# Output projection with odd-k weight buffers, early gate rows, samples' decays taken later; new beginning; operands at other SBUF addresses

## The chip, the cores and the metric

One Trainium2 chip, one of its cores. The metric is the device time of one launch in microseconds; the kernel before was run three times, and its time is the median of them.

## What is computed

One layer of a hybrid decoder, on 1024 prompt tokens and 8 samples of 8 tokens (T = 1088 columns in all), width D = 1024, everything in float32. Cut to what matters:

```python
mod = silu(c) @ w_ada + b_ada                     # (9, 6 * 1024): 1 prompt row, 8 sample rows
sh1, sc1, g1, sh2, sc2, g2 = split(mod, 6)
h = rms_norm(x, norm_mix_pre) * (1 + sc1) + sh1
proj = h @ w_in                                   # 6688 columns: z, x/B/C, dt, q, k, v, gate, beta, alpha
y = gated_rms_norm(ssd(causal_conv(x/B/C), dt))   # Mamba-2, 16 heads of 64, chunked scan
o = gated_rms_norm(delta_net(causal_conv(q, k, v), beta, alpha))   # 8 heads of 128
m = concat(y, o) @ w_out                          # 2048 x 1024
x = x + g1 * rms_norm(m, norm_mix_post)
h = rms_norm(x, norm_ffn_pre) * (1 + sc2) + sh2
f = (silu(h @ w_gate) * (h @ w_up)) @ w_down      # DFF = 2816
x = x + g2 * rms_norm(f, norm_ffn_post)
```

The samples start from given states and convolution halos; the prompt starts from zero. The new states are outputs too.

## The kernel before

**Precision.** Every large product is three matmuls: both operands are split into a rounded high part and a low rest (`hh`/`hl` or `sh`/`sl` for activations, `wh`/`wl` for weights), and high x high, low x high and high x low are summed in PSUM. `load_half` (L167 to L173) loads a 128x512 piece of weights `wr` on SP's DMA queue; `split_half` (L161 to L166) makes `wh` by a cast on ACT (L164) and `wl` by a subtraction on DVE (L165). Pool `wp` has four buffers of each.

**Stages.** (1) Start: the adaLN blocks 0, 2, 1, 3 of 512 columns (`ada_block`, L268), norm of the nine token tiles (`norm_x`), transposing and modulating into the hidden columns `hh`, `hl` in three groups TH of 384, 384 and 320 columns (`hidden`, L353; its transposes are L320), and the first two tiles of the input projection, K and Q, beside it (`first_half`, L401, matmuls L408 to L410; for the other groups L189 to L191). (2) The GDN stage to about 750 us, (3) the SSD stage to about 998 us: the input projection runs tile by tile (`gemm`, L185), with recurrences beside it. (4) w_out, 998 to 1268 us: `gemm_rows` (L1325) goes over three groups of three token tiles; for each k (8 to 15, then 0 to 7) it takes a piece of the mixed rows (`mixed_piece`, `mx`), splits it into `sh`, `sl`, loads two halves of w_out and issues 18 matmuls (L1335, L1337, L1338). (5) FFN-up, 1270 to 1720 us, in a Strassen-like scheme of seven block products (L1815 to L1817, 272 columns each; the blocks are allocated in `blocks`, L1580). (6) w_down, 1720 us to the end.

**Order of the work.** Side work is written as Python generators (`spawn`) that go on by a step at each `tick()`; `wait(n)` lets n ticks pass. A tick comes after some matmuls of the running tile, so `wait` sets behind how many matmuls something is issued. PE's order is the order in which the program text issues (a manual schedule on PE alone). The order on ACT, DVE, POOL and SP's queue is decided by a scheduler when the program is built, with `tc.high_priority` as a hint; each engine then executes its list in order.

**Side work the change touches.** `params`, `halos` (the convolution halos of the samples, L366; five loads through one buffer `vT`, transposed at L373), `rates` (decay rates; its first product is L522), `ada_rest` (L635): the other eight adaLN blocks during the GDN stage, whose sums go to DRAM (`pdr`). `rows_late` (L1274) reads `pdr` back in w_out and makes the gate rows `gaindr` (L1301) and the FFN's `modT` (L1313) from it. `decays(j)` (L1033) loads and exponentiates the decays `L` of SSD head pair j; `ssd_pair(j)` (L1052) calls it for j + 1 before its own `xd`, `xe` (L1073, L1074; matmul L1091). `gdn_samples` (L1409) does the eight delta-net heads of the samples beside w_out, after `rows_late` (`beside`). It begins with

```python
sp.dma_start(out=d0, in_=accr[16:24, NP:T].partition_broadcast(NS))
dve.tensor_tensor(out=d0, in0=d0, in1=acs[0:NS, NC, 16:24]...)      # L1423
dve.tensor_scalar(out=d0, in0=d0, scalar1=0.0, ...)                 # L1425
act.activation(out=d0, in_=d0, func=AF.Exp)                         # L1426
yield from wait(3)
```

where `d0` is `s_d` in the profile, and then for each head h loads the state S0 (`s_S`), builds the operand `kb`, issues the products `pk` (L1512) and `pw` (L1520), scales S0 by eight end decays on POOL (L1527), and issues the product `po` (L1530).

Of the kernel before, what the change touches and what calls it, by code (L numbers as in the profile page):

```python
# [16 lines left out]
P = 128  # L17
D = 1024
# [25 lines left out]
def hybrid_step(ctx: ExitStack, tc: tile.TileContext, x_p, x_s, c_p, c_s, st_ssd, st_ssdc, st_gdn, st_gdnc,  # L44
# [30 lines left out]
    pdr = tc.dram_tile([P, 4 * D], F32, name="pdr")  # L75
# [3 lines left out]

    ident = const.tile([P, P], F32, name="ident")  # L80
# [24 lines left out]
    sels = const.tile([P, 4, 9], F32, name="sels")  # L105
    for i in range(4):
        dve.tensor_tensor(out=sels[:, i, :], in0=fold[:, 0:9], in1=ident[:, 9 + i:10 + i].to_broadcast([P, 9]),
                          op=ALU.add)
# [59 lines left out]
    def load_half(src, low=dve):  # L168
# [4 lines left out]
        return split_half(wr, low)  # L173
# [82 lines left out]
    for i in range(3):  # L256
        load_x(i, act)
# [40 lines left out]

    def params():
        act.dma_start(out=r1[0:8, :], in_=n_mix_pre[0].rearrange("(r c) -> r c", c=P))  # L300
        act.dma_start(out=r1[8:16, :], in_=n_ffn_pre[0].rearrange("(r c) -> r c", c=P))
        act.dma_start(out=r1[16:24, :], in_=ssd_nw[0].rearrange("(r c) -> r c", c=P))
        act.dma_start(out=r1[24:25, :], in_=gdn_nw)
        act.dma_start(out=r1[25:37, :], in_=ssd_cb[0].rearrange("(r c) -> r c", c=P))
        act.dma_start(out=r1[37:85, :], in_=ssd_cw[0].rearrange("j (r c) -> (j r) c", c=P))
        act.dma_start(out=r2, in_=gdn_cw[0].rearrange("j (r c) -> (j r) c", c=P))
        yield from wait(3)
# [4 lines left out]
        dve.tensor_copy(prm2T, ps[:, 128:224])  # L312

# [39 lines left out]
    def hidden(g, step, ks=range(KD)):  # L353
        c0, n = TH[g]
        for k in ks:
            ps = turned(g, k)
            modulated(ps, k, c0, n, hh[k][:, c0:c0 + n], hl[k][:, c0:c0 + n], init,
                      pool if k % 2 else dve)
            if k % step == step - 1:
                yield  # L360
        if KD - 1 in ks:
            hid_box[g] = clock[0]


    def halos():
        for src, a, n in ((st_ssdc[0], 0, 8), (st_ssdc[0], 8, 4), (st_gdnc[0], 0, 8), (st_gdnc[0], 8, 8),  # L366
                          (st_gdnc[0], 16, 8)):
            st = gk.tile([P, NP], F32, name="vT", bufs=1)[0:24, 0:n * P]
            act.dma_start(out=st, in_=src[:, :, a * P:(a + n) * P].rearrange("b t c -> (b t) c"))
# [8 lines left out]

    def hidden_rest():
        for i in range(3, NT):  # L380
            norm_x(i)
        yield from wait(5)
        yield from hidden(1, 3)
        yield from hidden(2, 3)
# [1529 lines left out]
```

## Time and profile before

| | us |
|---|---|
| runs | 2026.26, 2027.66, 2016.43; median 2026.26 |
| the profiled execution | 2017.53 |
| its span | 2015.8 |
| PE busy | 1951.3 (97%) |
| VectorE (DVE) busy | 1356.6 (67%) |
| ScalarE (ACT) busy | 1014.1 (50%) |
| GpSimd (POOL) busy | 138.7 (7%) |
| mean granted TensorE clock | 0.99 of full |

The span is the stretch from the first to the last instruction; the execution's own time has 1.7 us more around it. PE is TensorE's matmuls, PEld its weight loads, SPq the queue on which the Sync engine issues DMAs. A line number is that of the kernel before; a matmul row reads `out<-stationary or moving operands`, and in brackets stands how long the engine was idle before an instruction and what released it.

### The profile page before, as it was taken

Reading aid. Unit: us, or ns where it says so; the run is one execution under the profiler, and the core shown is the slowest. Engines: PE = TensorE matmul, PEld = TensorE weight load, DVE = VectorE, ACT = ScalarE, POOL = GpSimd, SP = SyncE. Lnnn points to the kernel's source line nnn. Section 1 sums busy time; section 2 is a strip of 40 time slices with the busy share of each in tenths; the row PEclk is TensorE's granted clock in tenths of the full one; section 3 lists DMA queues with packets and bytes.
Section 4 is the critical chain, followed back from the end, with each engine's and each line's share of the span. In section 5 each row is a group of like instructions: output and inputs, shape, how many; then the busy total and the mean of one; then the engine's idle time right before and its main releaser. Section 6 shows DMA issues by size and latency. Waiting matters only on the chain.

```text
span 2015.8 us, 35469 instructions
## 1 busy us (share of the span) xinstructions
PE 1951.3 (97%) x13211; PEld 1752.5 (87%) x13211; DVE 1356.6 (67%) x2949; ACT 1014.1 (50%) x2515; POOL 138.7 (7%) x188
## 2 busy tenths in 40 slices
PE   6999999999999999999989999999999999999998
PEld 4888999999999998998857677899999999988886
DVE  4768677877887656867648777885555556645465
ACT  3555445555555447767424556753333334444454
POOL 2110000000000001010002210100000000000000
PEclk8999999999999999999989999999999999999999
DMA  9133223333221237545376866422222223633131
GB/s 315 40 92 92 84 92 98 108 95 99 84 58 55 69 92 201 159 121 155 113 218 193 253 203 194 140 75 81 73 78 81 75 82 124 225 125 113 46 100 50
DMA packets 224764, 239.49 MB, mean 119 GB/s; under 512 B 19128, under 2 KB 177387, under 8 KB 224461
## 3 DMA queue, kind: packets, MB, share of 16 engines
q1 hardware_dynamic: 218203, 231.88, 37.2%
q10 hardware_dynamic: 6386, 5.33, 0.8%
q8 instruction: 104, 1.70, 0.4%
q14 instruction: 71, 0.58, 0.1%
HBM read 190.93 MB, written 46.25 MB: 118 GB/s over the span
## 4 chain that ended last, share of the span: by engine, by line
PE 79%; DVE 9%; DMA 6%; ACT 3%; issue 2%; POOL 0%; SPq 0%; DVEq 0%; POOLq 0%; ACTq 0%
PE ps L189 8%; PE ps L190 8%; PE ps L191 8%; PE ps L1815 7%; PE ps L1817 7%; PE ps L1816 7%; PE ps L1335 7%; PE ps L1338 6%; PE ps L1337 6%; PE ps L671 2%; PE ps L725 1%; DMA L<-accr 1%; DVE tm L827 1%; DVE rr L829 1%; DMA mx<-mixdr 1%
## 5 line engine op out<-in xcount | busy, mean ns | idle before, releaser
L189 PE MATMUL ps<-hh,wh 128*128 128x384 f32 (+1 forms) x1232 | 436.2, 354 | 0.0
L190 PE MATMUL ps<-hl,wh 128*128 128x384 f32 (+1 forms) x1232 | 403.3, 327 | 0.0
L191 PE MATMUL ps<-hh,wl 128*128 128x384 f32 (+1 forms) x1232 | 403.3, 327 | 0.0
L1335 PE MATMUL ps<-wh,sh 128*128 128x512 f32 x678 | 275.2, 406 | 7.2 <-ACT wh L164 6.4
L1338 PE MATMUL ps<-wl,sh 128*128 128x512 f32 x678 | 267.3, 394 | 3.9 <-DVE wl L165 3.8
L189 PEld LDWEIGHTS ps<-hh,wh 128*128 128x128 f32 x1232 | 232.3, 189 | 16.8 <-issue 10.4
L1337 PE MATMUL ps<-wh,sl 128*128 128x512 f32 x604 | 238.9, 395 | 0.0
L190 PEld LDWEIGHTS ps<-hl,wh 128*128 128x128 f32 x1232 | 232.4, 189 | 0.8
L191 PEld LDWEIGHTS ps<-hh,wl 128*128 128x128 f32 x1232 | 231.3, 188 | 0.0
L164 ACT CAST wh<-wr 128x512 fp32r<-128x512 f32 x200 | 123.7, 621 | 183.0 <-PE ps L190 87.6
L165 DVE TENSOR_TENSOR wl<-wr,wh 128x512 fp32r<-128x512 f32 x200 | 137.6, 693 | 66.5 <-ACT wh L164 65.8
L1335 PEld LDWEIGHTS ps<-wh,sh 128*128 128x128 f32 x678 | 128.4, 189 | 49.7 <-issue 13.7
L165 DVE TENSOR_TENSOR wl<-wd,wh 128x512 fp32r<-128x512 f32 x130 | 89.6, 692 | 118.0 <-ACT wh L164 114.7
L1338 PEld LDWEIGHTS ps<-wl,sh 128*128 128x128 f32 x678 | 128.4, 189 | 35.2 <-DVE wl L165 6.3
L164 ACT CAST wh<-wd 128x512 fp32r<-128x512 f32 x130 | 80.7, 621 | 138.9 <-PE ps L1337 100.7
L1337 PEld LDWEIGHTS ps<-wh,sl 128*128 128x128 f32 x604 | 114.7, 190 | 21.3
L1815 PE MATMUL ps<-T_0h,wh 128*128 128x272 f32 x352 | 102.2, 290 | 4.3 <-DVE u L1831 1.8
L1752 ACT CAST wh<-s 128x512 fp32r<-128x512 f32 x104 | 64.3, 620 | 78.2 <-PE ps L1816 72.6
L1817 PE MATMUL ps<-T_0h,wl 128*128 128x272 f32 x352 | 102.0, 290 | 0.7 <-DVE wl L1753 0.7
L1815 PE MATMUL ps<-T_1h,wh 128*128 128x272 f32 x352 | 102.1, 290 | 0.0
L1816 PE MATMUL ps<-T_0l,wh 128*128 128x272 f32 x352 | 101.5, 288 | 0.0
L1817 PE MATMUL ps<-T_1h,wl 128*128 128x272 f32 x352 | 101.5, 288 | 0.0
(490 smaller groups left out, 4372.8 us busy)
## 6 DMA issues: line engine op xcount, KB each, us to landing
wr<-in_w_in_dram SPq DMA_DIRECT2D x104, 256.0 KB
wr<-in_w_gate_up_dram SPq DMA_DIRECT2D x104, 256.0 KB
wr<-in_w_out_dram SPq DMA_DIRECT2D x96, 256.0 KB
w<-in_w_ada_dram SPq DMA_DIRECT2D x16, 1024.0 KB
wd<-in_w_down_dram SPq DMA_DIRECT2D x22, 512.0 KB
actdr<-as SPq DMA_DIRECT2D x18, 544.0 KB
L<-accr SPq DMA_DIRECT2D x16, 544.0 KB
am<-actdr SPq DMA_DIRECT2D x44, 192.0 KB
```

The lines of the kernel that those rows point to most:

```text
L164: act.copy(wh, src)
L165: low.tensor_tensor(out=wl, in0=src, in1=wh.bitcast(F32), op=ALU.subtract)
L189: pe.matmul(out, lhsT=hi[k], rhs=xh[k], start=(k == 0), stop=False)
L190: pe.matmul(out, lhsT=hi[k], rhs=xl[k], start=False, stop=False)
L191: pe.matmul(out, lhsT=lo[k], rhs=xh[k], start=False, stop=(k == KD - 1))
L1335: pe.matmul(o, lhsT=sh[:, cs], rhs=wh, start=first, stop=False)
L1337: pe.matmul(o, lhsT=sl[:, cs], rhs=wh, start=False, stop=False)
L1338: pe.matmul(o, lhsT=sh[:, cs], rhs=wl, start=False, stop=last)
L1752: act.copy(wh, opa[p])
L1815: pe.matmul(o, lhsT=wh[:, cs], rhs=bh[:, m, :], start=(m == 0 and not on), stop=False, **on)
L1816: pe.matmul(o, lhsT=wh[:, cs], rhs=bl[:, m, :], start=False, stop=False, **on)
L1817: pe.matmul(o, lhsT=wl[:, cs], rhs=bh[:, m, :], start=False, stop=(m == 3), **on)
```

## The change

**The beginning.** All loads go to SP, in the order of use: the rows of c, x tiles 0 to 2, adaLN blocks 0 and 2, the first halves of K and Q, blocks 1 and 3, the second halves, the other x tiles, parameters, halos, rate weights. Loading (`load_ada`, `load_params`, `load_halos`) is written apart from use. The pool of `w2` buffers has 12 in place of 8, and the halos use it. A Silu on one element is issued at the very beginning. On PE the work of column group 0 stands among the blocks' products; the later groups go slice by slice (`first_group`): transpose of slice k, then the six matmuls of slice k - 2. **Rates** wait three ticks more. **`ada_rest`** computes gate rows and `modT` itself, a block at a time, without the way through `pdr`. **`decays`** is split into loading and computing; for pair 1 the computing is written after `xd`, `xe` of pair 0. **w_out:** mixed rows are loaded four ahead from two pools, the weights of odd k have their own pool `wo` of three buffers, `rows_late` and `gdn_samples` run beside each other, `gdn_samples` waits 16 ticks and its decays are written after the first transposes, the operand of head h + 1 is prepared ahead, S0 is scaled on ACT, and `pw` follows `pk` after two ticks. **Addresses:** `space` puts 128 B behind each `sh`, `sl` pair, and a block of FFN-up has rows of 288 columns, of which 272 are used.

```diff
+    warm = cA.tile([1, 1], F32, name="warm")
+    dve.memset(warm, 0.0)
+    act.activation(out=warm, in_=warm, func=AF.Silu)
...
+    def space(pool_, n, names, shape):
+        for name in names:
+            pool_.tile(shape, F32R, name=name)
+        pool_.tile([P, n], F32, name="space", bufs=1)
...
-    act.dma_start(out=cc[0:1, :], in_=c_p)
+    sp.dma_start(out=cc[0:1, :], in_=c_p)
...
+    def first_group(g):
+        pss = [ps_a.tile([P, 512], F32, name="ps")[:, 0:TH[g][1]] for _ in first]
+        for k in range(KD + 2):
+            if k < KD:
+                mod(g, k, turned(g, k))
+            if k >= 2:
+                first_k(g, k - 2, pss)
+                tick()
+        hid_box[g] = clock[0]
+        return pss
+
+    load_ada(0)
+    load_ada(2)
+    for load in loads:
+        load(0)
+    load_ada(1)
     rows = ada_block(0)
+    load_ada(3)
+    for load in loads:
+        load(1)
     for i in range(3):
         norm_x(i)
     rows2 = ada_block(2, lambda: ada_cols(0, rows))
+    tps = [turned(0, k) for k in range(4)]
     ada_cols(2, rows2)
-    first_half(0)
+    for k in range(4):
+        mod(0, k, tps[k])
     rows = ada_block(1)
-    rows2 = ada_block(3, lambda: ada_cols(1, rows))
+    for k in range(2):
+        first_k(0, k, first_ps)
+    ada_cols(1, rows)
+    for k in range(2, 4):
+        first_k(0, k, first_ps)
+    rows2 = ada_block(3)
     for i in range(3, NT):
         load_x(i)
+    load_params()
+    load_halos()
...
+    def few():
+        yield from wait(6)
+        yield from params()
+        yield from halos()
+        yield from rate_weights()
...
-        yield from wait(8)
+        yield from wait(11)
...
         for i in range(16):
-            yield from wait(13)
+            yield from wait(11)
...
+            yield from wait(3)
+            ps = bank()
+            if sec in (0, 3):
+                pe.matmul(ps[0:9], lhsT=sels[:, cb, :], rhs=pr, start=True, stop=True)
+                dve.tensor_tensor(out=g9, in0=ps[0:9], in1=g9, op=ALU.mult)
+                sp.dma_start(out=gaindr[sec // 3][:, 512 * half:512 * half + 512], in_=g9)
+                continue
...
-        box["next"] = decays(j + 1) if j + 1 < KD else None
+        box["next"] = load_decays(j + 1) if j + 1 < KD else None
+        if 0 < j < KD - 1:
+            decays(j + 1, box["next"])
...
+        if j == 0:
+            decays(1, box["next"])
         yield from wait(4)
...
+    space(stk, 32, ("sh", "sl"), [P, 384])
...
-        t = mxp.tile([P, 384], F32, name="mx", bufs=3)
+        t = (g_ if queue and k % 2 else mxp).tile([P, 384], F32, name="mx", bufs=3)
...
+    wo = ph_b.enter_context(tc.tile_pool(name="wo", bufs=3, side="right", reuse_waits="tile"))
...
-        dve.tensor_tensor(out=d0, in0=d0, in1=acs[0:NS, NC, 16:24].unsqueeze(2).to_broadcast([NS, HG, NS]),
-                          op=ALU.subtract)
-        dve.tensor_scalar(out=d0, in0=d0, scalar1=0.0, scalar2=None, op0=ALU.min)
-        act.activation(out=d0, in_=d0, func=AF.Exp)
-        dve.tensor_tensor(out=d0, in0=d0, in1=tri8[:, 0:NS].unsqueeze(1).to_broadcast([NS, HG, NS]), op=ALU.mult)
-        yield from wait(3)
+        yield from wait(16)
         for a in range(2):
...
+        dve.tensor_tensor(out=d0, in0=d0, in1=acs[0:NS, NC, 16:24].unsqueeze(2).to_broadcast([NS, HG, NS]),
+                          op=ALU.subtract)
+        dve.tensor_scalar(out=d0, in0=d0, scalar1=0.0, scalar2=None, op0=ALU.min)
+        act.activation(out=d0, in_=d0, func=AF.Exp)
...
-            pool.tensor_tensor(out=S0, in0=S0, in1=ge.to_broadcast([P, NB, P]), op=ALU.mult)
+            for b in range(NB):
+                act.activation(out=S0[:, b, :], in_=S0[:, b, :], func=AF.Copy, scale=ge[:, b])
...
-                d[s_][n] = pool_.tile([P, 4, HN], F32R, name=f"{n}_{s_}{w}")
+                d[s_][n] = pool_.tile([P, 4, HN + 16], F32R, name=f"{n}_{s_}{w}")[:, :, 0:HN]
...
-    spawn(beside())
+    spawn(rows_late())
+    spawn(gdn_samples())
...
-        return load_half(w_out[k * P:(k + 1) * P, hf * 512:hf * 512 + 512])
+        return load_half(w_out[k * P:(k + 1) * P, hf * 512:hf * 512 + 512], wp=wo if k % 2 else wp)
...
-            while "rows" not in late_box:
-                tick()
```

The order of instructions, at three places. A row is a line, an operation and its operands. First, SP's queue at the program's beginning (`w` is an adaLN buffer, `wr` a piece of w_in, `kq` a buffer that holds an x tile). Before:

```order
L274 DMA w_188<-in_w_ada_dram 128x2x512
...
L274 DMA w_240<-in_w_ada_dram 128x2x512
L172 DMA wr<-in_w_in_dram 128x4x128 x2
L274 DMA w_321<-in_w_ada_dram 128x2x512
...
L274 DMA w_358<-in_w_ada_dram 128x2x512
L172 DMA wr<-in_w_in_dram 128x4x128 x2
L246 DMA kq<-in_x_prompt_dram 128x1024
L246 DMA w_383<-in_x_prompt_dram 128x1024
```

Now:

```order
L234 DMA gate<-in_c_prompt_dram 1x1024
L235 DMA gate<-in_c_sample_dram 8x1024
L236 DMA gate<-in_norm_mix_pre_dram 1x1024
L255 DMA kq<-in_x_prompt_dram 128x1024 x3
L285 DMA w_193<-in_w_ada_dram 128x2x512
...
L285 DMA w_207<-in_w_ada_dram 128x2x512
L181 DMA wr<-in_w_in_dram 128x4x128 x2
L285 DMA w_221<-in_w_ada_dram 128x2x512
...
L285 DMA w_246<-in_w_ada_dram 128x2x512
L181 DMA wr<-in_w_in_dram 128x4x128 x2
L255 DMA kq<-in_x_prompt_dram 128x1024
```

The rows of c and three x tiles, which ACT's queue issued, now stand ahead of the sixteen adaLN pieces on SP; the second halves of K and Q and the other x tiles still stand behind all of them.

Second, DVE at the first SSD pair (L1044, now L1120, is the decays' step on `L`; `xd`, `xe` are what PE waits for). Before:

```order
L1073 TENSOR_TENSOR xd<-ps,dt 128x512
L1023 TENSOR_TENSOR bb<-btk,blkm 64x1024
L1044 TENSOR_SCALAR L<-L,rate_643 128x64
L1074 TENSOR_TENSOR xe<-ps,rate_643 128x512
L1073 TENSOR_TENSOR xd<-ps,dt 128x512
L1074 TENSOR_TENSOR xe<-ps,rate_643 128x512
L1044 TENSOR_SCALAR L<-L,rate_643 128x64
```

Now:

```order
L1150 TENSOR_TENSOR xd<-ps,dt 128x512
L1096 TENSOR_TENSOR bb<-btk,blkm 64x1024
L1151 TENSOR_TENSOR xe<-ps,rate_510 128x512
L1150 TENSOR_TENSOR xd<-ps,dt 128x512
L1151 TENSOR_TENSOR xe<-ps,rate_510 128x512
L1155 TENSOR_TENSOR xd<-ps,dt 64x128
L1157 TENSOR_TENSOR xe<-ps,rate_510 64x128
L1120 TENSOR_SCALAR L<-L,rate_510 128x64 x2
```

The decays' two steps have moved behind all of `xd` and `xe`.

Third, ACT in w_out around the Exp of the samples' decays (L1347, now L1398, casts mixed rows into `sh`; L164, now L173, casts weights into `wh`; L1436, now L1484, is the samples' work on the first transposes). Before:

```order
L1347 CAST sh<-mx 128x384
L164 CAST wh<-wr 128x512 x2
L1426 ACT_TABLE_LOAD
L1426 ACTIVATE s_d_11795<-s_d_11795 64x512
L1347 CAST sh<-mx 128x384
L164 CAST wh<-wr 128x512 x2
...
L1436 ACTIVATE jk,ssm<-ps 128x128 x8
```

Now:

```order
L173 CAST wh<-wr 128x512
L1257 ACTIVATE sz<-y 128x1088
L173 CAST wh<-wr 128x512
L1398 CAST sh<-mx 128x384 x3
L1492 ACT_TABLE_LOAD
L1492 ACTIVATE s_d_11581<-s_d_11581 64x512
L173 CAST wh<-wr 128x512 x4
L1398 CAST sh<-mx 128x384
L173 CAST wh<-wr 128x512 x2
```

The Exp stood behind the sixth `sh` cast of w_out and stands behind the fourth now, with four `wh` casts directly behind it.

## Rows read from the trace of the kernel before

**Rows 1.** The page, part 1: busy time, share and instructions of each engine.

```profile
PE 1951.3 (97%) x13211; PEld 1752.5 (87%) x13211; DVE 1356.6 (67%) x2949; ACT 1014.1 (50%) x2515; POOL 138.7 (7%) x188
```

**Rows 2.** Windows of the start: length, busy (count) by engine, granted clock, DMA share, GB/s.

```profile
0.00:20.00 20.00, 9.67 (x51) 3.52 (x51) 4.55 (x17) 5.86 (x8) 4.28 (x24) 1.00 0.93 343
20.00:40.00 20.00, 16.21 (x97) 11.42 (x98) 10.12 (x19) 5.73 (x11) 3.77 (x4) 0.83 0.96 294
40.00:60.00 20.00, 13.09 (x72) 10.60 (x70) 12.83 (x30) 11.71 (x23) 7.28 (x9) 0.74 0.69 196
```

**Rows 3.** Waits of PE: in total us, times, longest us.

```profile
PE ps L259 <- ACT gate L229: 7.5, 1, 7.5
PE ps L1335 <- ACT wh L164: 6.4, 2, 6.1
PE ps L373 <- DMA vT<-in_state_ssd_conv_dram: 4.5, 1, 4.5
PE ps L1338 <- DVE wl L165: 3.8, 2, 2.7
...
PE ps L409 <- DVE hl L349: 3.3, 2, 2.2
PE ps L1091 <- DVE xe L1074: 3.0, 1, 3.0
PE ps L522 <- DVE s L516: 2.3, 1, 2.3
...
PE ps L1313 <- DMA rows<-pdr: 1.0, 1, 1.0
```

**Rows 4.** Windows around four holes, and of FFN-up.

```profile
776.00:782.00 6.00, 5.34 (x35) 4.91 (x36) 5.96 (x16) 5.94 (x16) 1.09 (x1) 0.72 0.61 151
1030.00:1038.00 8.00, 8.00 (x25) 3.85 (x25) 1.90 (x4) 0.00 (x0) 0.00 (x0) 0.79 0.29 91
1045.00:1050.00 5.00, 5.00 (x15) 3.89 (x15) 4.87 (x9) 3.32 (x9) 0.00 (x0) 0.50 0.89 286
1242.00:1246.00 4.00, 4.00 (x12) 3.09 (x12) 4.00 (x8) 0.76 (x2) 0.00 (x0) 0.59 0.78 251
1400.00:1500.00 100.00, 100.00 (x799) 100.00 (x798) 57.13 (x103) 38.21 (x80) 0.00 (x0) 1.00 0.25 79
```

**Rows 5.** Timeline of PE at the start: start us, us, line, instruction, wait.

```profile
36.54 1.06 PE L268 MATMUL ps<-w,caF 128*32 128x512 f32 x8
...
82.80 0.34 PE L189 MATMUL ps<-hh,wh 128*128 128x384 f32 x1
```

**Rows 6.** Timeline of ACT at the start.

```profile
5.01 1.28 ACT L229 ACT_TABLE_LOAD   x1 [5.01 <-DMA gate<-in_c_sample_dram]
```

**Rows 7.** Timeline of SP in w_out.

```profile
1003.10 0.32 SPq L1173 DMA_DIRECT2D mixdr<-y  x1
...
1037.28 0.63 SPq L1420 DMA_DIRECT2D s_d<-accr  x1
```

**Rows 8.** Timeline of all engines in w_out, at the samples' decays.

```profile
1040.26 0.68 DVE L1423 TENSOR_TENSOR s_d<-s_d,rate 64x512 f32<-64x512 f32 x1 [3.32 <-DMA s_d<-accr]
...
1041.43 0.63 ACT L1426 ACTIVATE s_d<-s_d 64x512 f32<-64x512 f32 x1 [17.82 <-DVE s_d L1425]
```

**Rows 9.** Timeline of PE at w_out's first matmuls.

```profile
998.76 0.50 PE L1335 MATMUL ps<-wh,sh 128*128 128x512 f32 x1
...
1003.00 0.39 PE L1335 MATMUL ps<-wh,sh 128*128 128x512 f32 x1
```

**Rows 10.** The line L1156: its form, count, shortest, median and longest ns.

```profile
L1156 ACT ACTIVATE h<-h,eb x64: 385/390/414, 786.8 to 994.9; 128x128 f32<-128x128 f32 x64
```

**Rows 11.** Timeline of PE in FFN-up.

```profile
1501.56 0.29 PE L1815 MATMUL ps<-T_0h,wh 128*128 128x272 f32 x1
...
1501.94 0.29 PE L1815 MATMUL ps<-T_1h,wh 128*128 128x272 f32 x1
...
1502.31 0.29 PE L1815 MATMUL ps<-T_1h,wh 128*128 128x272 f32 x1
```

More of the change, by code (lines that the diff above doesn't have):

```diff
@@ L103, in hybrid_step @@
     dve.tensor_add(fold, fold, ident[:, 96:128])
-    sels = const.tile([P, 4, 9], F32, name="sels")
-    for i in range(4):
+    sels = const.tile([P, 8, 9], F32, name="sels")
+    for i in range(8):
         dve.tensor_tensor(out=sels[:, i, :], in0=fold[:, 0:9], in1=ident[:, 9 + i:10 + i].to_broadcast([P, 9]),
@@ L268, in ada_rows, with load_ada @@
             pe.matmul(ps[r], lhsT=caF[:, k, :], rhs=w(k), start=k < 4, stop=k >= 4)
+    w2s = {}
+    def load_ada(cb):
+        w2s[cb] = []
+        for k in range(0, KD, 2):
+            w2 = init.tile([P, 2, 512], F32, name="w2", bufs=12)
+            sp.dma_start(out=w2, in_=w_ada[k * P:(k + 2) * P, cb * 512:(cb + 1) * 512]
+                         .rearrange("(a p) n -> p a n", p=P))
+            w2s[cb].append(w2)
     def ada_block(cb, between=None):
@@ L351, in hybrid_step, with mod, load_halos @@
     hid_box = {}
-    def hidden(g, step, ks=range(KD)):
+    def mod(g, k, ps):
         c0, n = TH[g]
[L355 to L362, printed above, removed]
+        modulated(ps, k, c0, n, hh[k][:, c0:c0 + n], hl[k][:, c0:c0 + n], init, pool if k % 2 else dve)
+    HALOS = ((st_ssdc[0], 0, 8), (st_ssdc[0], 8, 4), (st_gdnc[0], 0, 8), (st_gdnc[0], 8, 8), (st_gdnc[0], 16, 8))
+    sts = []
+    def load_halos():
+        for src, a, n in HALOS:
+            st = init.tile([P, 2, 512], F32, name="w2", bufs=12).rearrange("p a n -> p (a n)")[0:24, 0:n * P]
+            sp.dma_start(out=st, in_=src[:, :, a * P:(a + n) * P].rearrange("b t c -> (b t) c"))
+            sts.append(st)
     def halos():
[L366 to L369, printed above, removed]
+        for st, (src, a, n) in zip(sts, HALOS):
             ps = bank()
@@ L377, in halos @@
         hid_box["halos"] = clock[0]
[L379 to L384, printed above, removed]
     def tile_halves(c0):
@@ new lines, in hybrid_step, with rate_weights @@
+    tps = [turned(0, k) for k in range(4, KD)]
+    ada_cols(3, rows2)
+    for k in range(4, KD):
+        mod(0, k, tps[k - 4])
+    with tc.high_priority(-80):
+        for i in range(3, NT):
+            norm_x(i)
+    for k in range(4, KD):
+        first_k(0, k, first_ps)
+    hid_box[0] = clock[0]
+    wst = gk.tile([P, NP], F32, name="gate")[:, 0:KD * 64].rearrange("p (k m) -> p k m", m=64).bitcast(F32R)
+    def rate_weights():
+        pool.memset(wst.bitcast(F32), 0.0)
+        act.copy(wst[:, :, 0:32], wsr)
+        dve.tensor_sub(wst[:, :, 32:64], wsr, wst[:, :, 0:32].bitcast(F32))
+        yield
@@ L1267, in hybrid_step @@
     late_box = {}
+    KS = list(range(KD, 2 * KD)) + list(range(KD))
+    queue, last = [(k, *TH[gi]) for gi in range(2) for k in KS], []
+    for i in range(4):
+        ahead.append(mixed_load(*queue.pop(0)))
     def load_gains(i, gp, gs):
@@ L1274, in rows_late @@
     def rows_late():
-        def rows(s):
-            r = pre.tile([P, D], F32, name="rows2", bufs=2)
-            sp.dma_start(out=r, in_=pdr[:, s * D:(s + 1) * D])
-            return r
-        r0, r1_ = rows(0), rows(1)
         while "norm" not in rate_box:
@@ L1400, in piece @@
         def piece(k):
-            m = ahead.pop(0) if ahead else mixed_load(k, c0, n)
+            m = ahead.pop(0)
+            if queue or last:
+                ahead.append(mixed_load(*(queue or last).pop(0)))
             if k < KD:
@@ L1505, in gdn_samples @@
             dve.tensor_tensor(out=diag(1), in0=bt(smp[:, h, 1, :]), in1=bt(eg[:, h, :]), op=ALU.mult)
-            yield from wait(1)
+            return S0, kb
+        nxt = prep(0)
+        yield from wait(2)
+        for h in range(HG):
+            S0, kb = nxt
             pk = bank()
```

179 lines of the change are left out of this document (77 added, 102 removed).

## Prediction

> **What bounds the kernel now.** I read the page first. PE is busy for 1951.3 of 2015.8 us [rows 1], so 64.5 us are idle; whatever the change does must shorten those holes, shorten PE's own instructions, or lose. Second view: the start by windows [rows 2]. In the first 40 us the DMA engines are 0.93 and 0.96 busy while PE is half idle: the start waits for bytes. From 40 to 60 us DMA falls to 0.69, PE is still idle for a third, and the granted clock is 0.74: with two levels, 2.4 and 1.2 GHz, a mean of 0.74 means that 52% of the stretch ran at the low one. Third view: the waits of PE [rows 3], which name the holes: the gate 7.5 us, `wh` in w_out 6.4, `vT` 4.5, `wl` in w_out 3.8, `hl` 3.3, `xe` 3.0, `s` in the rates 2.3. They lie at a few places, not all along, so each can be followed in its own timeline. Fourth: the windows around the holes [rows 4], because a hole costs twice. The matmuls behind it run at the low level: 0.72 in 776 to 782 us, 0.79 in 1030 to 1038, 0.50 in 1045 to 1050, 0.59 in 1242 to 1246.
>
> **The start.** The chain is: bytes of the four adaLN blocks, then their products, then the hidden columns, then the first two tiles. In the trace the last block's products begin at 36.54 us and the first two tiles end where the next tile's L189 begins, at 82.80 [rows 5]. The change puts every load into SP's queue in the order of use. Ahead of the last block's end stand then three x tiles (1.57 MB), four blocks (8.39 MB) and half of K and Q (0.52 MB), 10.5 MB, with the other x tiles and all small loads behind them. At the rates of the windows, 343 GB/s for 20 us (6.86 MB) and 294 GB/s after that [rows 2], they have landed at 20 + 3.64/0.294 = 32.4 us, at 343 throughout at 30.6: I take 31.5, so 5.0 us sooner. The gate's 7.5 us are gained only in part: the warm activation takes the table load of 1.28 us at 5.01 [rows 6] away from it, but PE then waits for bytes anyway, so I count nothing for it. The 4.5 us of PE behind `vT` [rows 3] go: the five halo loads no longer share a buffer one after another, and their transposes come six ticks after the first group. The 3.3 us behind `hl` [rows 3] go for a third, since `mod` is now issued four slices ahead: 1.0. Sum: -10.5 us. Bounds: -5 if only the bytes come sooner; -16 if also all of `hl` and the low clock of 40 to 60 us go (52% of 20 us at half speed is 5.2 us). PE still has the same products to do behind the last block, so more cannot go. What may be late next is x3 to x8 behind 10.5 MB, which were issued on SP in the kernel before at about the time of the last block too.
>
> **Rates.** `wait(8)` becomes `wait(11)`: three ticks, each some matmuls long, cover a wait of 2.3 us [rows 3]. -2.3 (0 to -2.5).
>
> **First SSD pair.** DVE stands with the decays of the next pair, which wait for a DMA, ahead of `xe`; the order shows them behind it now. PE's 3.0 us [rows 3] go, and with them the clock: 0.72 over 6 us [rows 4] is 56% at half speed, 1.7 us. What is queued behind the moved pieces is `wl` of the next tile, which another tile's products cover. -4.5 (0 to -4.7).
>
> **Gate rows.** 16 + 4 products and 64 narrow ones are the same before and after; they move from w_out into the GDN stage, so 0. PE's hole behind `rows<-pdr` lies in the next term.
>
> **w_out, the samples' decays.** In the trace `s_d` is issued on SP at 1037.28 [rows 7], DVE starts at 1040.26 after 3.32 us of waiting for it, and ACT's Exp starts at 1041.43 after 17.82 us of standing still [rows 8]. All `wh` casts stand behind that Exp. PE pays 6.4 us [rows 3], then the low clock: 0.50 over 5 us is 2.5, and about 0.6 in the windows beside it, so 3.1. With the `rows<-pdr` episode before it (0.79 over 8 us [rows 4], 42% at half speed, 1.7; the wait itself 1.0 [rows 3]) the stretch costs 12.2. The program text writes the decays later, but the order of ACT shows the Exp still *early*: behind the fourth `sh` cast, ahead of four `wh` casts. On SP `s_d` stands two weight halves, two mixed tiles and `smx` behind the store of `y`, which is issued at 1003.10 [rows 7]. I put its issue at 1006.2, its landing 3.0 later (1037.28 to 1040.26), DVE's two steps and the Exp 1.8, the cast behind them 0.6: 1011.6. PE has weights for k = 8 and 9, 36 matmuls from 998.76 at 0.236 (18 of them lie between the rows 998.76 and 1003.00 [rows 9]), and one transpose group: until about 1008. So the old hole dies but a **new** one of 3.6 us takes its place, with some 2.0 of low clock. Net 12.2 - 5.6 = -6.6; bounds 0 hole (-12.2) and a hole as dear as the old (-2.7).
>
> **w_out, weights.** Odd-k halves in their own three buffers put 7 halves ahead in place of 4. The 3.8 us behind `wl` [rows 3] and the clock of 1242 to 1246 (0.59 over 4 us, 1.6 us [rows 4]) come where ACT and DVE do the norms of finished rows beside the casts. Three more halves are 9 matmuls of 0.236 each, 6.4 us of cover, but the same order of ACT and DVE: I take half, -2.7 (0 to -5.4).
>
> **S0's scaling** goes from POOL to ACT, eight 128x128 copies a head at 0.39 us (the nearest row, L1156 [rows 10]): 3.1 us a head, 25 in all. Hidden by those halves; if the cover goes, each head can stop the casts (a rival below). 0.
>
> **Addresses.** A block row in FFN-up was 272 columns, 1088 B, and becomes 288, 1152 B, a multiple of 128; the products are the same. The trace shows one product of three matmuls beginning 0.38 after another (1501.56 to 1501.94) and the next 0.37 after that (to 1502.31) [rows 11]; 799 matmuls in 100 us [rows 4] are 0.3755 a triple. [...] With 0.3725 for all, 3 ns less in some 1200 triples (450 us at that rate): -3.6; bounds 0 and -6.6 (0.37). The same for the input projection, w_out and w_down isn't shown by rows: 0, give or take 2. A rule speaks against this term. The Trainium skill, "TensorE: Matmul & The Clock Gate", Part 2, says that PE reads its streaming operand and its weights through two independent ports of SBUF, so that a weight load takes no bandwidth from a running matmul. By that rule, addresses change nothing and the sum is 3.6 us smaller; the alternating 0.37 and 0.38 speak against it, if weakly, at the rows' 0.01 us.
>
> **Sum:** -10.5 - 2.3 - 4.5 - 6.6 - 2.7 - 3.6 = -30.2, from 2017.53 for the profiled execution to 1987.3. That execution stands 8.7 us under the median of the three runs (2026.26), near their lowest; I add a third of it, 2.9: **1990 us**.
>
> **Rivals.**
> (a) *The addresses do nothing:* the 0.01 us between the triples has another cause, and the blocks' new spacing leaves FFN-up at 799 matmuls per 100 us. All else as above: 1987.3 + 3.6 + 2.9 = 1994. Chance 0.20. The rule of the Trainium skill's TensorE page, above, is on this side.
> (b) *Given back.* The decays don't move, as ACT's order hints: the new hole costs the old one's price (-2.7 in place of -6.6), `wl` gains nothing, and at the start only the bytes come sooner (-5). Then -5 - 2.3 - 4.5 - 2.7 - 3.6 = -18.1: 2002. For it: one FIFO puts x3 to x8, which every later slice needs, last. Chance 0.20.
> (c) *Slower: ACT stops in every head.* S0's copies wait for PE's products of that head and stand ahead of `wh` casts on ACT, an engine that executes in order. Where ACT reaches them early, the casts stop, PE runs dry and the clock falls: the price of one such event is that of the Exp, 6.1 + 3.1 = 9.2 us. Eight heads are 74 us: 2061. It decides from the fifth head on, since 30.2 + 10 is 4.4 such events. Against it: POOL did the same wait without harm, and 7 halves ahead are 15 us of products (9 matmuls of 0.236 each), against 3.1 us of ACT a head. Chance 0.05.
> (d) *More goes than I count:* the start at its bound (-16), w_out without a hole (-12.2, -5.4): -44, 1976. Chance 0.12.
>
> **How the numbers follow.** My forecast has 0.43. The range leaves out (c) and the ends of the rest: 1970 to 2010. About 0.5%, 10 us, is what a measurement of this kernel can tell from no change, since its three runs spread over 11 us. Against 2026 that is 2016: the forecast, (a), (d) and most of (b) lie below it, 0.89; same 0.07; slower 0.04.
>
> **What would show it.** Right: the first tile behind the first two begins at about 72 in place of 82.8; no PE wait on `vT` or `rows<-pdr`; no wait on `xe` over 1 us; a wait of 2 to 5 us on `wh` near 1000 (in the new time) with a low clock behind it; FFN-up at over 803 matmuls per 100 us. Wrong: a start that still ends near 80; waits on `wh` in the heads' stretch; FFN-up at 799.

## The result and the profile after

Six runs of each kernel on one chip: the changed kernel 2012.78 us in the median (2010.51 to 2016.55), the kernel before 2025.5 (2016.43 to 2027.66). The ratio is 0.9945, with a 95% interval of 0.9929 to 0.996: **faster by half a per cent**, where 1990 us and a ratio of 0.982 had been forecast, and outside the range. The sign was right, two thirds of the gain are missing. The two profiled executions, 2017.53 and 2012.82 us, stand only 4.8 apart, because that of before stands near its kernel's fastest run (2016.43); differences of times within the traces, below, are between these two.

The waits of PE in the changed kernel (total us, times, longest us):

```profile
PE ps L1386 <- ACT wh L173: 15.2, 1, 15.2
...
PE ps L1388 <- DVE sl L1399: 3.7, 1, 3.7
...
PE ps L417 <- DVE hl L368: 3.2, 3, 1.6
...
PE ps L1202 <- DVE hS L1181: 1.7, 1, 1.7
...
PE ps L416 <- ACT hh L367: 1.2, 1, 1.2
...
PE ps L1171 <- DVE xe L1151: 0.2, 1, 0.2
```

One row is as large as all gains: 15.2 us behind `wh` in w_out. The holes that the change aimed at are gone or smaller: `xe` 0.2 in place of 3.0, `vT` and `rows<-pdr` no longer appear [rows 3]. But `hS` (1.7) has taken over from `xe`, and `sl` (3.7) from `wl` in the last group of w_out.

Windows of the changed kernel (length, busy and count by engine, granted clock, DMA share, GB/s):

```profile
20.00:40.00 20.00, 16.84 (x109) 11.23 (x108) 10.83 (x20) 7.83 (x13) 3.42 (x3) 1.00 1.06 376
40.00:60.00 20.00, 17.19 (x87) 16.17 (x87) 13.34 (x27) 12.12 (x22) 8.96 (x12) 0.83 0.39 90
60.00:80.00 20.00, 18.43 (x93) 13.68 (x91) 9.70 (x33) 6.86 (x16) 2.70 (x3) 0.68 0.02 3
1000.00:1020.00 20.00, 7.69 (x51) 4.96 (x50) 10.70 (x16) 7.25 (x14) 0.00 (x0) 0.82 0.81 242
1400.00:1500.00 100.00, 100.00 (x801) 100.00 (x800) 56.06 (x100) 38.79 (x82) 0.00 (x0) 1.00 0.25 78
```

Against [rows 2] the DMA engines are fuller in 20 to 40 us (1.06 at 376 GB/s, 294 before), and PE is busier from 40 to 60. But 60 to 80 us run at a granted clock of 0.68, so 64% of it at the low level. 1000 to 1020 us is mostly hole. FFN-up does 801 matmuls per 100 us, before 799 [rows 4].

PE of the changed kernel at two marks of the beginning (the last adaLN block's products; the first tile behind the first two):

```profile
32.54 1.92 PE L277 MATMUL ps<-w,caF 128*32 128x512 f32 x16
...
87.06 0.45 PE L198 MATMUL ps<-hh,wh 128*128 128x384 f32 x1
```

The two rows of the last block don't mark the same place: 36.54 in [rows 5] begins the second half of its products, 32.54 all of them. Their ends compare: 37.60 before, 34.46 now, so 3.1 us sooner. The first two tiles nevertheless end 4.3 us *later* (82.80 in [rows 5]), so 7.4 us are lost behind the last block.

PE of the changed kernel at the beginning of w_out and of FFN-up:

```profile
1003.46 0.51 PE L1386 MATMUL ps<-wh,sh 128*128 128x512 f32 x1
...
1007.47 0.40 PE L1389 MATMUL ps<-wl,sh 128*128 128x512 f32 x1
1023.07 0.79 PE L1386 MATMUL ps<-wh,sh 128*128 128x512 f32 x1 [15.20 <-ACT wh L173]
```

```profile
1266.94 0.29 PE L1873 MATMUL ps<-B_0h,wh 128*128 128x272 f32 x1
```

and the kernel before at FFN-up's beginning:

```profile
1267.93 0.29 PE L1815 MATMUL ps<-B_0h,wh 128*128 128x272 f32 x1
```

w_out begins 4.7 us behind the kernel before (998.76 in [rows 9]); PE does 18 matmuls, all of k = 8, and stops for 15.2 us. At FFN-up's first matmul the changed kernel is 1.0 ahead, at the end of the spans (2015.8 and 2011.0) 4.8.

| stage | forecast, us | measured, us |
|---|---|---|
| beginning, to the end of the first two tiles | -10.5 | +4.3 |
| GDN and SSD stages (rates, `xe`, and the gate rows' products moved in) | -6.8 | +0.4 |
| w_out (and the gate rows' products moved out) | -9.3 | -5.7 |
| FFN-up and w_down | -3.6 | -3.8 |
| sum | -30.2 | -4.8 |

The middle two rows belong together, since the gate rows' products leave one for the other: -16.1 forecast, -5.3 measured. Two errors make the difference: 14.8 us at the beginning and 10.8 in these two. These are differences of single traces: the GDN and SSD stages, the same program in the changed kernel and in all twelve experiments, take 911.2 to 919.7 us in their traces (before: 916.0), so the second row is good to some us only. The first is firmer: the next tile begins at 86.4 to 88.2 us in the five traces with the changed beginning and at 82.8 to 84.7 in the three with the old one.

### The profile page after: what moved, and what is told of

Read it like the earlier page. It is cut to its first block, busy times and chain, and to the rows that moved or that the text cites. A ratio compares the mean times of both kernels' runs of the same rounds, so it can differ in the third digit from the quotient of the medians.

```text
span 2011.0 us, 35475 instructions
## 1 busy us (share of the span) xinstructions
PE 1951.5 (97%) x13211; PEld 1753.8 (87%) x13211; DVE 1351.1 (67%) x2964; ACT 1035.2 (51%) x2578; POOL 125.9 (6%) x184
## 4 chain that ended last, share of the span: by engine, by line
PE 84%; DVE 6%; ACT 3%; DMA 3%; issue 2%; SPq 1%; POOL 1%; DVEq 0%; POOLq 0%; ACTq 0%
PE ps L198 9%; PE ps L199 8%; PE ps L200 8%; PE ps L1874 7%; PE ps L1873 7%; PE ps L1875 7%; PE ps L1386 7%; PE ps L1389 7%; PE ps L1388 6%; PE ps L741 2%; PE ps L795 1%; DMA wr<-in_w_out_dram 1%; PE ps L704 1%; DVE uc L891 1%; DMA L<-accr 1%
## 5 line engine op out<-in xcount | busy, mean ns | idle before, releaser
L198 PE MATMUL ps<-hh,wh 128*128 128x384 f32 (+1 forms) x1200 | 425.6, 355 | 0.1
L200 PE MATMUL ps<-hh,wl 128*128 128x384 f32 (+1 forms) x1200 | 393.0, 327 | 0.0
L199 PE MATMUL ps<-hl,wh 128*128 128x384 f32 (+1 forms) x1200 | 392.6, 327 | 0.0
L1386 PE MATMUL ps<-wh,sh 128*128 128x512 f32 x678 | 274.6, 405 | 16.0 <-ACT wh L173 15.2
L198 PEld LDWEIGHTS ps<-hh,wh 128*128 128x128 f32 x1200 | 227.1, 189 | 17.1 <-issue 11.5
L199 PEld LDWEIGHTS ps<-hl,wh 128*128 128x128 f32 x1200 | 227.3, 189 | 0.8
L200 PEld LDWEIGHTS ps<-hh,wl 128*128 128x128 f32 x1200 | 226.0, 188 | 0.0
L173 ACT CAST wh<-wr 128x512 fp32r<-128x512 f32 x200 | 122.7, 621 | 171.0 <-PE ps L199 84.5
L173 ACT CAST wh<-wd 128x512 fp32r<-128x512 f32 x130 | 80.7, 621 | 139.0 <-PE ps L1388 100.3
L1874 PE MATMUL ps<-T_1l,wh 128*128 128x272 f32 x352 | 101.6, 289 | 0.0
```

What stands on the lines that cost most here:

```text
L173: act.copy(wh, src)
L198: pe.matmul(out, lhsT=hi[k], rhs=xh[k], start=(k == 0), stop=False)
L199: pe.matmul(out, lhsT=hi[k], rhs=xl[k], start=False, stop=False)
L200: pe.matmul(out, lhsT=lo[k], rhs=xh[k], start=False, stop=(k == KD - 1))
L1386: pe.matmul(o, lhsT=sh[:, cs], rhs=wh, start=first, stop=False)
L1874: pe.matmul(o, lhsT=wh[:, cs], rhs=bl[:, m, :], start=False, stop=False, **on)
```

## The experiments

Each is an edit of the changed kernel. They ran on three chips, on which the kernel before took 2023.4 to 2027.0 us beside them, so single times are compared to some us only. Two questions: why does PE stop in w_out, and what eats the beginning's gain? The first has two candidates, and their rows lie side by side. SP, then ACT, in the changed kernel:

```profile
1004.87 0.39 SPq L1246 DMA_DIRECT2D out_dram<-h  x1
...
1012.39 0.64 SPq L1473 DMA_DIRECT2D s_d<-accr  x1
...
1015.64 1.07 SPq L181 DMA_DIRECT2D wr<-in_w_out_dram  x2
```

```profile
1013.81 0.92 ACT L1398 CAST sh<-mx 128x384 fp32r<-128x384 f32 x2 [4.67 <-DMA mx<-mixdr]
...
1021.50 0.63 ACT L1492 ACTIVATE s_d<-s_d 64x512 f32<-64x512 f32 x1 [3.83 <-DVE s_d L1491]
1022.40 1.28 ACT L173 CAST wh<-wr 128x512 fp32r<-128x512 f32 x2 [0.27 <-DMA wr<-in_w_out_dram]
```

The Exp of the samples' decays (`s_d`) ends at 1022.13 us, and the cast that PE waits for follows it. That is the old culprit, as the forecast feared (theory E). But the cast itself waited 0.27 us more for its *weights*. ACT's list has the casts of k = 8, 10 and 12 ahead of the Exp and those of k = 9 and 11 behind it. In the program text the new pools open only behind the close of the SSD stage's, whose last state `h` is stored at 1004.87; on SP's queue the load of the weights of k = 9 then stands behind `s_d` and others, at 1015.64. That is theory L: the operands of odd k come late. (That their buffers lie on `h` itself is not shown: no row has the load wait for that store.)

**e1: the Exp out of the way.** The load of `s_d` is written where it is used.

```diff
-        sp.dma_start(out=d0, in_=accr[16:24, NP:T].partition_broadcast(NS))
...
+        sp.dma_start(out=d0, in_=accr[16:24, NP:T].partition_broadcast(NS))
         dve.tensor_tensor(out=d0, in0=d0, in1=acs[0:NS, NC, 16:24]...
```

> Edit to the changed kernel: the load of the samples' decays is written where they are used, so the Exp leaves the head of ACT's list in w_out; weights and mixed rows as changed. Theory E (the Exp holds the casts): the hole of 15.2 us at the first matmul of k = 9 falls below 4 us, about 11 us off the time. Theory L (the operands of odd k come late, because their new buffers lie in memory that the SSD stage gives back last): the weights of k = 9 land when they did, at 1022 us less what one small load took of the queue, so the hole stays at 13 us or more and the time within 3 us of the changed kernel.

One run: 2015.45 us. Waits of PE, and ACT's time line:

```profile
PE ps L1386 <- ACT wh L173: 14.8, 1, 14.8
```

```profile
1013.22 1.34 ACT L1398 CAST sh<-mx 128x384 fp32r<-128x384 f32 x3 [4.73 <-DMA mx<-mixdr]
1021.31 1.35 ACT L173 CAST wh<-wr 128x512 fp32r<-128x512 f32 x2 [6.76 <-DMA wr<-in_w_out_dram]
```

No Exp stands there, and the hole is still 14.8 us. The cast waits 6.76 us for its weights. Theory E falls.

**e2 and e3: the operands of the first odd k from the old pools.**

```diff
-        return load_half(..., wp=wo if k % 2 else wp)
+        return load_half(..., wp=wo if k % 2 and (gi or k not in (9, 11)) else wp)
```

and in e3 also

```diff
-        t = (g_ if queue and k % 2 else mxp).tile([P, 384], F32, name="mx", bufs=3)
+        t = (g_ if queue and k % 2 and len(queue) < 30 else mxp).tile([P, 384], F32, name="mx", bufs=3)
```

> Edit to the changed kernel: the weights of k = 9 and 11 of the first group come from the old pool again; the Exp and the mixed rows as changed. Theory L: the weights are there, but the mixed rows of k = 9 also have a new buffer and landed at 1013.8 us, so PE's first hole, between k = 8 and k = 9, falls from 15.2 to about 7 us. Theory E: the Exp at 1021.5 us still holds the casts behind it, so a hole of 9 us or more stays, now behind k = 9.

> Edit to the changed kernel: the weights of k = 9 and 11 and the mixed rows of k = 9 in the old pools; the Exp still written and listed early. Theory L: no hole over 3 us before k = 10, and less than 4 us in all around the Exp, since its load now stands behind fewer late transfers. Theory E: PE runs through k = 8, 9 and 10 on casts made before the Exp and then stops until the casts behind it: a hole of 5 us or more behind k = 10. Both theories: time lower than that of the changed kernel, by 12 to 18 us under L, by 6 to 10 under E.

e2 took 2008.55 us, e3 1997.91. The hole of e2, in its waits of PE:

```profile
PE ps L1386 <- ACT sh L1398: 6.5, 1, 6.5
```

It is now `sh`, the mixed rows of k = 9, that come late: their new buffer lies in a pool that also opens behind the SSD stage. With both in the old pools no wait on `wh` or `sh` is left; the longest of PE's in w_out is one on the samples' transposes:

```profile
PE ps L1504 <- DVE s_ko L1485: 2.4, 1, 2.4
```

and ACT of e3 makes the casts before the Exp in time and loses nothing behind it:

```profile
1017.95 0.62 ACT L173 CAST wh<-wr 128x512 fp32r<-128x512 f32 x1 [1.44 <-PE ps L1388]
...
1020.53 0.63 ACT L1492 ACTIVATE s_d<-s_d 64x512 f32<-64x512 f32 x1 [0.65 <-DVE s_d L1491]
```

So the hole was two late operands, one behind the other, and not the Exp. Both expectations of theory L came true (6.5 us for 7, then none over 3). Other traces repeat it: from w_out's first matmul to the end of the span, the five with both late operands (the changed kernel, e1, e4, e8, e9) take 1007.5 to 1013.6 us, the six with both in the old pools and the new pool for the rest (e3, e5, e6, e7, e10, e12) 993.4 to 1003.5.

**e4, e6, e7: the beginning.** e4 takes the narrow halo transposes out from between the slices of the last column group (`few` waits 16 ticks instead of 6), e6 puts them into the second group (0 ticks).

> Edit to the changed kernel: the parameters, halos and rate weights are no longer interleaved with the slices of the last column group but come in one piece behind it. Theory H (the narrow 24-wide transposes between the slices keep TensorE's clock at its low level from 67 to 84 us): the granted clock of 65 to 80 us rises from 0.50 to 0.72 to over 0.9, and the next tile begins at 78 to 81 us in place of 87.1, some 7 us off the time. Rival (the clock falls at the waits of up to 1.6 us at the turn to the last group and comes back on its own): the clock stays at 0.5 for over 10 us behind the turn, and the next tile begins at 85 us or later.

> Edits to the changed kernel: odd-k operands as in e5; parameters, halos and rate weights start with the first slice of the second column group instead of six slices later. Theory H (narrow transposes between the slices bring the clock down wherever they stand): the low clock moves to the second group, 50 to 62 us, and the last group, 65 to 80, runs at 0.9 or more; the next tile begins at 81 to 86. Rival (the turn to the last group brings it down): 65 to 80 us stays at 0.5 to 0.7 as in the changed kernel.

e4 took 2008.75 us, e6 (with e3's edits) 2004.17. One window of 65 to 85 us in the kernel before and in the changed kernel, then windows of e4 and of e6:

```profile
65.00:85.00 20.00, 20.00 (x126) 18.34 (x125) 13.45 (x38) 10.30 (x26) 4.04 (x7) 1.00 0.13 29
```

```profile
65.00:85.00 20.00, 19.16 (x84) 15.27 (x85) 10.62 (x37) 5.83 (x16) 2.70 (x3) 0.57 0.11 27
```

```profile
65.00:70.00 5.00, 5.00 (x23) 4.27 (x23) 2.81 (x9) 1.67 (x5) 1.56 (x2) 0.66 0.00 0
70.00:75.00 5.00, 3.94 (x23) 2.96 (x22) 3.97 (x10) 2.49 (x6) 1.16 (x2) 1.00 0.24 66
75.00:80.00 5.00, 4.42 (x35) 3.78 (x34) 2.27 (x8) 2.46 (x11) 0.86 (x1) 1.00 0.14 39
80.00:85.00 5.00, 5.00 (x34) 4.95 (x33) 3.71 (x15) 3.40 (x8) 0.72 (x3) 0.51 0.79 260
```

```profile
55.00:60.00 5.00, 5.00 (x41) 4.40 (x41) 3.39 (x8) 1.34 (x2) 1.51 (x2) 0.96 0.02 3
60.00:65.00 5.00, 5.00 (x40) 4.43 (x39) 3.84 (x9) 1.64 (x3) 1.51 (x2) 1.00 0.00 2
...
70.00:75.00 5.00, 5.00 (x18) 4.02 (x18) 1.84 (x5) 1.13 (x3) 0.87 (x1) 0.50 0.00 0
```

The kernel before runs this stretch at 1.00, the changed kernel at 0.57, so 17 of the 20 us at the low level. In e4 that ends by 70, 70 to 80 run at 1.00, and the low level comes back behind the 36 halo transposes, in a shorter piece:

```profile
79.15 3.35 PE L391 MATMUL ps<-ident,w 24*128 24x24 f32 x36
82.43 0.69 PE L198 MATMUL ps<-hh,wh 128*128 128x384 f32 x1
```

The next tile begins at 82.43, 4.6 us sooner than at 87.06, where theory H wanted 6 to 9. About 2 of these are given back behind this mark, where the low level runs on to some 87 us. In e6 the narrow transposes do no harm in the second group (0.96 and 1.00), and 70 to 75 us are at 0.50 without any, with 0.90 and 0.92 in the windows beside it: neither H's 0.9 nor the rival's 0.5 to 0.7. Its next tile begins at 85.19. So the low stretch begins behind the turn to the last group wherever the narrow transposes stand, as the rival has it, and taking them out of that group shortens it from 17 us to 3 (e4) or 7 (e6), as H has it. Why they prolong it there and not in the second group isn't shown.

e7 lets the transposes run four slices ahead instead of two (with e3's and e4's edits).

```diff
-        for k in range(KD + 2):
+        for k in range(KD + 4):
...
-            if k >= 2:
-                first_k(g, k - 2, pss)
+            if k >= 4:
+                first_k(g, k - 4, pss)
```

> Edits to the changed kernel: as e5, and the transposes of the later column groups go four slices ahead of the matmuls instead of two. Theory S (what eats the start's gain is the chain transpose, modulate, split, matmul, which two slices do not cover): PE's waits on hh and hl from 45 to 80 us fall from some 5 us to under 2, and the next tile begins at 79 us or earlier (82.4 in e4). Rival (the wait is at the turn of a group, where no earlier matmuls are left to cover it, whatever the distance): waits of 3 us or more stay and the next tile begins at 81 to 83.

One run: 1992.84 us. The next tile begins at 80.30, between the two expectations, and waits of 3.6 us on `hh` and `hl` remain from 45 to 80 us, as the rival has it; e7 does not decide between them.

**e5: both repairs together**, in four runs.

> Edits to the changed kernel: the weights of k = 9 and 11 of the first group and the mixed rows of k = 9 in the old pools, and parameters, halos and rate weights in one piece behind the last column group. Theory L + H: the two gains lie in stages 900 us apart and add, some 15 and 4 us: 1992 to 1997 us, a ratio to the kernel before of 0.982 to 0.988. Rival (part of the gain of either run was the spread of single runs, 6 us): 1998 to 2004.

Ratio 0.986 [0.982, 0.990], as expected; but the four runs spread from 1995.23 to 2006.66 us, with a median of 2003.35, on the rival's side. The next tile of its trace begins at 84.09, with the beginning of e4 (82.43). Single runs are good for time lines, not for totals of 5 us.

**e8: the blocks' old rows**, of 272 columns (`HN + 16` undone).

> Edit to the changed kernel: the blocks of FFN-up have rows of 272 columns again; nothing else. Theory A (the operands' distance modulo 128 B sets the 3 ns between triples): FFN-up goes back from 801 matmuls per 100 us to 799, over 450 us 1 us or a little more; time 1 to 2 us higher, which a single run cannot show. Rival (the rate has another cause): 801 stays.

2012.98 us, and the window of FFN-up:

```profile
1400.00:1500.00 100.00, 100.00 (x795) 100.00 (x794) 54.99 (x98) 38.27 (x81) 0.00 (x0) 1.00 0.24 76
```

795, less than either kernel; the changed kernel and the experiments that keep its rows have 801 in this window. So where the operands lie does matter, by 6 matmuls in 801 or 3 us over 450. But e8 has the rows of 1088 B of the kernel before with its 799, so the row length alone does not set the rate: neither theory A (799) nor its rival (801) came true.

**e9: the old beginning**, the rest as changed.

> Edit to the changed kernel: the whole beginning up to the end of the first two tiles is that of the kernel before (queues, order on PE, halos, norms); everything behind it as changed. Theory N (the new beginning is slower than the old one by itself): the next tile begins at 82 to 84 us instead of 87.1, and the profiled execution is some 4 us under that of the changed kernel, about 2008. Rival (something placed behind it, such as other buffers or the later work already queued, makes the start slow): the next tile still begins at 86 us or later.

2006.93 us; the next tile, and the wait in w_out:

```profile
82.93 0.34 PE L195 MATMUL ps<-hh,wh 128*128 128x384 f32 x1
```

```profile
PE ps L1342 <- ACT wh L170: 15.9, 1, 15.9
```

82.93, as in the kernel before (82.80): theory N holds, and the new beginning by itself costs 4.1 us. The late operands cost the same behind either (15.9).

**e10: one pipeline over two groups.** `first_group` runs each group by itself; here the slices of groups 1 and 2 are one sequence, four ahead (with e3's and e4's edits).

```diff
+    def first_groups():
+        seq, pss = [(g, k) for g in (1, 2) for k in range(KD)], None
+        for i in range(len(seq) + 4):
+            if i < len(seq):
+                mod(*seq[i], turned(*seq[i]))
+            if i >= 4:
+                g, k = seq[i - 4]
+                if k == 0:
+                    pss = [ps_a.tile([P, 512], F32, name="ps")[:, 0:TH[g][1]] for _ in first]
+                first_k(g, k, pss)
+                tick()
+                if k == KD - 1:
+                    hid_box[g] = clock[0]
+                    yield g, pss
```

> Edits to the changed kernel: as e5 (odd-k operands of the first k in the old pools, halos behind the last group), and the slices of the second and third column group run in one sequence, four slices ahead of the matmuls across the turn. Theory S (the turn between groups, where no matmul covers the chain of the first slice, makes the hole and the low clock behind it): no wait over 0.6 us and a granted clock of 0.9 or more from 60 to 75 us; the next tile begins at 76 to 79 us (80.3 in e7); time 1988 to 1996 us, a ratio of 0.980 to 0.985 to the kernel before. Rival (the hole moves to the PSUM banks that the last group gets only when the second group's are copied out): a wait of 1 us or more at the turn stays and the next tile begins at 80 us or later.

1996.28 us in the median of five runs, ratio 0.9849 [0.9828, 0.987]. Its windows, its waits from 45 to 79 us, and the next tile:

```profile
55.00:60.00 5.00, 2.73 (x15) 2.17 (x15) 3.32 (x6) 1.24 (x2) 3.45 (x4) 1.00 0.00 0
...
65.00:70.00 5.00, 5.00 (x32) 4.07 (x30) 3.88 (x13) 2.83 (x8) 0.86 (x1) 1.00 0.00 0
70.00:75.00 5.00, 4.00 (x25) 3.53 (x25) 3.53 (x9) 2.17 (x6) 2.06 (x2) 1.00 0.35 94
```

```profile
PE ps L339 <- DVE w L263: 2.3, 2, 1.4
PE ps L417 <- DVE hl L368: 1.3, 1, 1.3
PE ps L339 <- DVE rs L123: 1.1, 1, 1.1
PE ps L417 <- POOL hl L368: 1.0, 1, 1.0
```

```profile
78.75 0.69 PE L198 MATMUL ps<-hh,wh 128*128 128x384 f32 x1
```

The clock stays at 1.00 from 55 to 75 us, and the last group's first matmul (65.64) has no wait in front of it. Three of the four waits lie before 60 us, where the norms of the later x tiles (`w`, L263) come late; the fourth, 1.00 us on POOL's `hl`, stands in front of 73.49, at the last group's end, where theory S wanted none over 0.6. 78.75: theory S holds for the turn. All nine traces that keep the turn (the changed kernel, e1 to e8) have low clock behind it, e10 and e11 have none. e10 is the fastest version run more than once.

**e11 and e12: what the new weight pool buys, and the old beginning with the repair.** e11 is e10 with all weights from the old pool (`wp=wp`); e12 is e9 with e3's edits.

> Edit to e10: all weights of w_out come from the old pool of four; the new pool for odd k is not used at all. If the three more halves ahead buy what the prediction counted for them (2.7 us, from waits on wl in the last group), this is 2 to 3 us slower than e10 and waits on wl or wh of 2 us or more come back between 1180 and 1250 us. Rival (they buy nothing, because the casts stand in the same order on ACT and DVE whatever is loaded): the same as e10 within 1.5 us.

> Edits to the changed kernel: the old beginning (as in e9), and the weights of k = 9 and 11 and the mixed rows of k = 9 in the old pools (as in e3). If the new beginning's loss (87.1 against 81.6 us, 5.5) and the late operands' (15) are all that separates forecast and result, this gives 2012.8 - 5.5 - 15 = 1992, and 1990 to 1996 with the spread of runs; it is then level with e10 (1996) or some us better. Rival (the old beginning gives back elsewhere, in the stage behind it): 1997 or more.

e11: 2002.11 us, ratio 0.9893 [0.9872, 0.9915], outside e10's interval. Waits of PE in w_out and behind it in e11, then in e10:

```profile
PE ps L1390 <- ACT wh L173: 2.8, 1, 2.8
PE ps L1393 <- DVE wl L174: 2.7, 2, 1.6
PE ps L1877 <- ACT u L1889: 2.6, 2, 1.4
```

```profile
PE ps L1392 <- DVE sl L1403: 2.7, 1, 2.7
...
PE ps L1393 <- DVE wl L174: 1.6, 1, 1.6
```

Waits of 2.8 on `wh`, 1.1 more on `wl` and 2.6 on FFN-up's first `u` come back, one of 2.7 on `sl` goes; the first two lie between 1180 and 1250 us, as expected. e11 stands 5.8 us above e10 in the medians, 8.9 by the ratios. So once its first use is late enough, the pool does save time. That it saves more than the 2.7 counted for it is not shown: from w_out's first matmul to the end e11 takes 1004.8 us and e10 998.7, but the six traces with the new pool spread from 993.4 to 1003.5. e12: 1999.79 us, ratio 0.9879 [0.9861, 0.9897]: over the expected 1990 to 1996, on the rival's side; the sum had been built from single runs. It stands 3.5 us above e10 in the medians, with intervals that overlap, and its next tile begins at 84.72, 6.0 us later.

## Why the prediction was wrong

**The beginning (-10.5 forecast, +4.3 measured): the failed step is "PE still has the same products to do behind the last block", taken as if they would run as before.** `vT` went. But in the old order the later groups' hidden columns were made beside the matmuls of the first group; `first_group` puts each slice's transpose, its work on ACT and DVE, and its matmuls into one chain with two slices of lead. At each turn nothing covers the first slice. The waits there are small, the largest 1.6 on `hl` and 1.2 on `hh`, and all waits behind the last block are no longer than before (6.9 us, 8.2 before); but the stretch behind the last turn ran mostly at 1.2 GHz: 17 us at half speed from 65 to 85 are about 8.6 us. Over all of 40 to 85 us, by windows of 5 us, the low clock takes 11.9 us now and 5.1 before, and these 6.8 are nearly the whole of the 7.4 lost there. I had counted a clock gain at this place as a bound and no clock loss. `hl` gave nothing of the 1.0: 3.6 us of waits, 3.3 in [rows 3].

The bytes' term (-5.0) was misread too. It set the landing of 10.5 MB against 36.54, but PE came to that row from other work:

```profile
32.79 2.78 PE L268 MATMUL ps<-w,caF 128*32 128x512 f32 x24
```

```profile
PE ps L268 <- DMA w<-in_w_ada_dram: 1.7, 2, 1.4
```

The 24 are block 1 and the first half of the last block, with no wait in front, and the old beginning waits 1.7 us for adaLN bytes in all, before 16 us. What the block gained, 3.1 us, would not have counted by itself in the old order: in e9 its products end 2.0 us later than before (39.64), and the next tile still begins at 82.93, because PE then waits for `vT` in either, to 54.04 before and to 54.13 in e9.

**w_out (-6.6 and -2.7 forecast): the failed step is "PE has weights for k = 8 and 9".** The new hole was foreseen, near 1000 us, on `wh`, with a low clock behind; its size was 3.6 us in the sum and 15.2 on the chip, and its cause was not the Exp. I had read from the order where the Exp stands, and not which halves of the weights are cast before it, nor when the new pools' first loads can be issued. The 11.6 us too little are more than the whole of what w_out and the stages before it lack (10.8).

**The weights' term** (-2.7) did not show in the changed kernel, where 3.7 us on `sl` stood in place of 3.8 on `wl` [rows 3]; behind the repair e10 and e11 show it, at a size that stays open.

**First SSD pair** (-4.5): the wait on `xe` went and its low clock too, but the moved decays stand ahead of `hS` on DVE now and wait there for the same DMA, 1.7 us of PE.

**Addresses** (-3.6): FFN-up gained 2 matmuls in 799, 1.1 us over 450, where 3.6 was taken; the rest of that stage's -3.8 are waits at its beginning. The failed step is "With 0.3725 for all": no run shows this term. Sorted by slice of a block (0 to 3), the triples from 1410 to 1700 us take 374, 377, 375 and 382 ns in the median before, 378, 373, 378 and 373 in the changed kernel and 374, 383, 375 and 382 in e8. So they still go by turns though the rows are now a multiple of 128 B long; the even slices became slower and the odd ones quicker. The Trainium skill, "TensorE: Matmul & The Clock Gate", Part 2, says that loading the next weights takes no SBUF read bandwidth from the running matmul; of operand addresses it says nothing. Read as in the prediction, it would give one rate for all spacings, and the traces do not agree (795, 799 and 801); whether weight loads have a part in that isn't shown.

**Rates** went as forecast: the wait on `s` is 0.2 in place of 2.3 us. **Rival (c)** did not come: no `wh` wait in the heads' stretch stands among the larger waits. **The range:** it held cases in which one term fails; here the beginning and w_out failed together.

## What to carry to other kernels

When a change gives some operands a new pool, ask first from when on its memory is free, and where the first load then stands on its queue: a deeper prefetch can begin later than the shallow one it replaces (here at 1015.64, 12 us behind w_out's first matmul); let the first uses keep the old buffers. When work is cut into a chain of short steps with a fixed lead, look at the turns, where the lead is zero, and price the low clock behind each wait with it. Read a hole's cause from the row that was last for each operand, not from the instruction that stands in front.

## What the runs showed of the hardware that was not expected

Waits of 0.8 to 1.2 us at the turn to the last group were followed by a granted clock of 0.50, 1.2 GHz, for some 3 us in e4 and 7 in e5, e6 and e7, and for some 17 us in the five traces (the changed kernel, e1, e2, e3, e8) in which narrow 24-column transposes stood between the matmuls that came next. The same transposes between the matmuls of the second group (e6, 55 to 65 us) left it at 0.96 to 1.00. In e10 a window with PE busy for only 2.73 of 5 us was followed by no fall at all. And one program differs from run to run: behind the 36 transposes, which stand alike in e10 and e11, the clock from 75 to 85 us was 0.85 and 0.80 in e10 and 1.00 in e11. What decides this was not tried further.

FFN-up's rate with unchanged matmuls was 795, 799 or 801 per 100 us, by where the operands lie, and its triples took 373 to 383 ns by the slice they read; which property of the addresses it is stays open.
